# Raw weight tiles fetched by transfers that GpSimd issues instead of SP

## The chip, the cores and the metric

The kernel runs on one core of a Trainium2 chip. The metric is the device time of one execution in microseconds (us). The core has TensorE (PE in the profile; PEld is its weight load), VectorE (DVE), ScalarE (ACT), GpSimd (POOL) and SyncE (SP). Each of them takes its own instructions strictly in order and waits on semaphores for the others. A transfer between HBM and SBUF is an instruction in the queue of the engine that issues it; the data is then moved by 16 DMA engines that all queues share.

## The reference

A small encoder trunk of two layers is run on two requests, of 1024 and 512 tokens, with one set of weights, all in float32.

```
def attn_retention_layer(x, g, w_in, qk_gain, ret_decay, w_out):
    z = rmsnorm(x, g) @ w_in
    qa, ka, va, ga, qb, kb, vb, gb = jnp.split(z, cuts, axis=-1)
    ...
    oa = dense_gqa(qa, ka, va)                         # mixer A, after norm and rotary
    ob = rmsnorm(fwd + bwd, None)                      # mixer B, retention in both directions
    mixed = jnp.concatenate([jax.nn.silu(ga) * oa, jax.nn.silu(gb) * ob], axis=-1)
    return x + mixed @ w_out
def windowed_layer(x, g, w_in, sink, rel_bias, w_out):
    z = rmsnorm(x, g) @ w_in
    q, k, v, gate = jnp.split(z, [...], axis=-1)
    o = banded_sink_gqa(q, k, v, sink, rel_bias)       # mixer C, +-128 tokens
    return x + (jax.nn.silu(gate) * o) @ w_out
```

The trunk applies the first layer, then the second, then a last RMS norm.

## The kernel before, in words

The 1536 tokens are 12 blocks of 128, in three groups t of four blocks (512 tokens). Activations stay in SBUF with the model dimension on the partitions, as a high part and a low part (tiles `xh` and `xl`, 8 of each per group, float32r). The weights are split the same way, and a product is three matmuls: high times high, high times low, low times high.

A weight matrix comes from HBM in chunks of 256 output columns. `load_w` (line 130) fetches one chunk in four pieces. For each piece it takes a raw tile `wraw` of 128 x 512 float32 (256 KB, 2 buffers in all), starts a transfer into it (line 134), makes the high part on GpSimd (line 136) and the low part (line 137) into a tile `w` or `wg`. The low part is made on GpSimd, except where the caller passes `lo=nc.vector`: then on VectorE. Once line 137 has read the raw tile, its buffer is free for the next transfer but one. There are 44 chunks, so 176 raw tiles.

Transfers of nearly everything else go through SP too: loads of activations, of residuals and of parked results (`mo`, `y`, `yn`, `xr`), and stores of gates, branch outputs and results. Twelve transfers, the keys and values of the attention, are issued by GpSimd already (lines 760 and 416).

In order of time (of the profiled execution):
- 0 to 116 us: the input is loaded and scaled (GpSimd scales groups t = 1 and 2 into `xh`, line 107), then the key, value and query projections of mixer A, with rotary steps on GpSimd (lines 103 and 394).
- 116 to 310: mixer B.
- 310 to 810: attention of mixer A; the scores of later blocks run beside the products of earlier ones, and between them fill matmuls of the gate projections (`psg`), from about 617 us on of the output projection of groups 2 and 0 (`pso`, function `out_proj_fm`). There GpSimd also multiplies branch output by gate (`mo`, line 259), sums squares (`acc`, line 282), and from about 740 us scales group 2 (`yn`, line 805).
- 810 to 887: the output projection of group 1 (`out_proj`, low parts on VectorE) and the key and value projection of mixer C.
- 887 to 1310: attention of mixer C with its query and gate projections as fill.
- 1310 to 1542: output projection of layer 1 (low parts on VectorE throughout), first beside the last attention units, from about 1430 us alone, and the final norm.

What stands in which order on each engine is decided when the program is built: a scheduler places every instruction by its own estimate of durations and by priorities, and it gives each tile a buffer. So one edit shifts rows all over the program. Between engines only semaphores decide.

Of the kernel before, what the change touches and what calls it, by code (L numbers as in the profile page):

```python
# [36 lines left out]
def trunk_kernel(ctx, tc, x, xT, wab, woab, wc, woc, gT, qkg, ret, sink, relb, fng,  # L37
                 ropeA, ropeB, dist, kdist, qdist, onehot, wmask, out_p0, out_p1, out_s):
    nc = tc.nc
    dma = nc.sync.dma_start  # L40
# [12 lines left out]
    def buf(tag, name, n=None, dt=F32):  # L53
        t = wk.tile([P, SIZE[tag]], dt, tag=tag, name=name, bufs=BUFS[tag])
        return t if n is None else t[:, :n]
# [74 lines left out]
    def load_w(arr, c, tag, lo=None, hook=None, ks=range(KT)):  # L130
        ts = {}
        for i in (k // 2 for k in ks[::2]):
            raw = wp.tile([P, 2 * CW], F32, tag="wraw", name="wraw", bufs=2)
            dma(out=raw, in_=arr[c, :, 2 * i:2 * i + 2, :].rearrange("p k n -> p (k n)"))
            w = wp.tile([P, 2, 2 * CW], F32R, tag=tag, name=tag, bufs=4)
            nc.gpsimd.tensor_scalar(w[:, 0, :], raw, 1.0, 1.0, ALU.mult, ALU.mult)  # L136
            (lo or nc.gpsimd).tensor_tensor(w[:, 1, :], raw, w[:, 0, :].bitcast(F32), ALU.subtract)  # L137
            ts[i] = w
            if hook is not None:
                hook(i)  # L140

        def get(s, k, a=0, n=CW):
            o = (k % 2) * CW + a
            return ts[k // 2][:, s, o:o + n]
        return get
# [76 lines left out]
    def gate_stream(warr, c0, gd, scale=None):  # L222
        for c in range(4):
            w = load_w(warr, c0 + c, "wg")
            for t in ORDER:
                for j in range(2):
                    yield from gate_pieces(w, j, 2 * c + j, t, gd, scale)
# [35 lines left out]
    def out_proj_fm(t, warr, ks, res, dst, finish, prev, lo):  # L263
        acc = buf("T", "acc")
        for c in range(4):
            w = load_w(warr, c, "w", lo, None, ks)
            for a in range(2):
                k = 2 * c + a
                y, sq = stage("y")
                dma(out=y, in_=res(k))  # L270
                ps = ps_p("pso")
                for kk in ks:
                    proj_fm_k(ps, w, a * P, t, kk, ks)
                    if kk != ks[-1]:
                        yield
                for side in ahead[:1] + (prev or []):
                    next(side, None)
                nc.vector.tensor_tensor(y, ps, y, ALU.add)
                dma(out=dst[k][t], in_=y)
                nc.scalar.activation(sq if k else acc, y, AF.Square)  # L280
                if k:
                    nc.gpsimd.tensor_tensor(acc, acc, sq, ALU.add)
                yield
# [32 lines left out]
    def out_proj(t, warr, ks, res, finish):  # L316
        x1 = [load_block(res(t * GB + j), "xr") for j in range(GB)]
        for c in range(4):
            with tc.high_priority():
                w = load_w(warr, c, "wg" if c % 2 else "w", nc.vector, None, ks)  # L320
            for j in range(GB):
                ps = ps_any("pso")[:, :CW]
                proj_tm(ps, w, t * GB + j, ks)
                sl = x1[j][c // 2][:, (c % 2) * CW:(c % 2 + 1) * CW]
                with tc.high_priority():
                    nc.vector.tensor_tensor(sl, ps, sl, ALU.add)
        finish(t, x1)
# [10 lines left out]
    sp_d = {(n, g, i): dr.tile([P, 1024 if i == 0 else 512], F32, name=f"sp{n}{g}{i}")[:]  # L338
            for n in ("ak", "av", "ch", "cl", "cv") for g in range(2) for i in range(2)}

# [1 line left out]
    ident = const.tile([P, P], F32, name="ident")  # L342
    make_identity(nc, ident)
    nhalf = const.tile([P, 8], F32, name="nhalf")
# [16 lines left out]
        for b in range(t * GB, t * GB + GB):  # L361
            block_rstd(load_block(x[b], "xb", "H"), rs[:, b:b + 1])

# [1 line left out]
    dma(out=g_sb, in_=gT)  # L365
    nc.scalar.activation(rs, rs, AF.Tanh)
    wkv = load_w(wab, 4, "w", None, lambda i: [load_xt(0, k) for k in ((0, 1), (2, 3, 4, 5), (6, 7), ())[i]])
# [127 lines left out]
        if p % 2:  # L495
            kv_group(p // 2)

# [1 line left out]
    ropeb = buf("S4", "ropeb").rearrange("p (f b d) -> p f b d", f=2, b=8)  # L499
    dma(out=ropeb, in_=ropeB)  # L500
    qdec = buf("S4", "qdec").rearrange("p (h a i) -> p h a i", h=4, a=2)
# [116 lines left out]
            tail, last = retention(h, w, b0, b1), tail  # L618
            last()

# [1 line left out]
    class Back:  # L622
        def __init__(self, eget, n, vget, od, k0, t, j, gd):
            self.n, self.eget, self.vget, self.od, self.k0, self.t, self.j = n, eget, vget, od, k0, t, j
# [46 lines left out]
                split(X["h", k, self.t][:, sl], X["l", k, self.t][:, sl], oT[:, a, :], 0.5)  # L671

    def pipeline(units, prep, front, cap, frees, rate, fill, hook, before=None):
        """Software pipeline: the scores of later units run beside the products of this one, as far as
        the buffers of the exponentials (cap of them) reach."""
        n = len(units)
        st_ = dict(u=0, gen=None, live=0)
        ctxs, backs, pend = {0: prep(units[0])}, {}, []

        def advance():  # L680
            u = st_["u"]
            if u >= n:
                return False
            if st_["gen"] is None:
                st_["gen"] = front(units[u], ctxs.pop(u))
                if u + 1 < n:
                    ctxs[u + 1] = prep(units[u + 1])
                st_["need"] = next(st_["gen"])
            if st_["live"] + st_["need"] > cap:
                return False  # L690
            st_["live"] += st_["need"]
            try:
                st_["need"] = next(st_["gen"])
            except StopIteration as e:
                backs[u] = e.value
                st_["u"], st_["gen"] = u + 1, None
            return True

        credit = 0.0
        for u in range(n):  # L700
            while u not in backs:
                advance()
                if before is not None and backs:
                    before()
                    before = None
            back = backs.pop(u)
            for kb in range(back.n):
                back.T(kb)
                st_["live"] -= frees(kb, back.n)
                credit = min(credit + rate(back.n), 4.0)  # L710
                while credit >= 1.0 and advance():
                    credit -= 1.0
                fill.step()
                for f in pend:
                    f()
                pend = [lambda bk=back, kb=kb: bk.PV(kb)]
                if kb == 0:
                    hook(units[u])
        for f in pend:
            f()  # L720
# [79 lines left out]
                    lambda kb: load_a("av", g, b)[:, kb * P:(kb + 1) * P], o_ab, 2 * g, t, j,  # L800
                    g_ab if g == 1 and t < 2 else None)

# [1 line left out]
    def fin_fm(t, k, y, rb):  # L804
        nc.gpsimd.tensor_tensor(y, y, rb, ALU.mult)
        split_x(y, k, t, g_sb[:, KT + k:KT + k + 1])
# [43 lines left out]

    out_proj(1, woab, KS_A, lambda b: x[b], fin_ab)

# [1 line left out]
    wkv = load_w(wc, 0, "w")  # L854
    kd_raw = {}
    for p in PAIRS:
# [34 lines left out]
            split(q[r0:r0 + 64], q[r1:r1 + 64], ps[r0:r0 + 64], 0.125)  # L891
        yield

# [1 line left out]
    k_c, v_c = {0: (KH, KL)}, {0: (V,)}  # L895
    qs = {}
    bias_c = {}
# [104 lines left out]
        return Back(lambda h, kb: es[h][:, kb * P:(kb + 1) * P], k1 - k0, lambda kb: vget_c(c, k0 + kb), o_c, 2 * c, t, j,  # L1002
                    g_c if (c, t) == (3, 1) else None)

# [1 line left out]
    def fin_out(t, k, y, rb):  # L1006
        nc.vector.scalar_tensor_tensor(y, y, g_sb[:, 2 * KT + k:2 * KT + k + 1], rb, ALU.mult, ALU.mult)
        dma(out=(out_p0, None, out_s)[t][k], in_=y)
# [126 lines left out]
```

## Time and profile before

| | |
|---|---|
| median of three runs | 1546.78 us (1539.06, 1546.78, 1547.49) |
| span of the profiled execution, first to last instruction | 1541.9 us (its whole time is not listed apart from the three runs) |
| busy PE / PEld | 1467.9 us (95%) / 1277.2 us (83%) |
| busy DVE / ACT / POOL | 1061.1 (69%) / 714.0 (46%) / 804.7 us (52%) |
| transfers | 179.54 MB, mean 116 GB/s |
| raw weight tiles | 176 transfers of 256 KB, all issued by SP, 3.2 to 3.6 us from issue to landing |
| granted TensorE clock, mean | 0.985 |

Busy shares are means over stages with different limits. DMA-issuing instructions are not counted as busy time, those on GpSimd neither, although one of them holds the engine for as long as it lasts.

### The profile page before, as it was taken

To read this page: it belongs to the slowest core of one execution; us is meant where nothing else is said; L and a number is where in the kernel's file an instruction comes from. 1 tells how busy PE (TensorE), PEld (TensorE's weight loads), DVE (VectorE), ACT (ScalarE), POOL (GpSimd) and SP (SyncE) were. 2 spreads that over 40 slices of the span, in tenths; PEclk is the share of its full clock that TensorE was granted. 3 is DMA by queue.
4 is the path that set the end of the run, shared out by engine and by line. 5 is a ranking of instruction groups with operands and counts; after the bars stand their busy time and mean duration, and the time that the engine had idled before them with its cause. 6 is when DMAs were issued, how large, how long until landed. Compare 5 with 4: busy or idle time off the path is not lost.

```text
span 1541.9 us, 26034 instructions
## 1 busy us (share of the span) xinstructions
PE 1467.9 (95%) x8746; PEld 1277.2 (83%) x8746; DVE 1061.1 (69%) x2488; ACT 714.0 (46%) x1768; POOL 804.7 (52%) x1040
## 2 busy tenths in 40 slices
PE   7989999989999999999998999999999999988897
PEld 7988999987888888778777998888888888766677
DVE  6596455578667667877888327677777767898554
ACT  3632222245455555655653235556556556555102
POOL 7783334257456374887896414442522432567433
PEclk9998999999999999999999999999999999999999
DMA  9441011224421132654563422112213211567773
GB/s 334 155 154 52 19 45 49 64 85 140 138 73 59 48 110 73 217 166 130 153 218 115 124 78 78 52 57 56 80 49 93 61 53 52 169 211 235 242 247 123
DMA packets 112662, 179.54 MB, mean 116 GB/s; under 512 B 12880, under 2 KB 34000, under 8 KB 112528
## 3 DMA queue, kind: packets, MB, share of 16 engines
q1 hardware_dynamic: 110512, 172.37, 35.6%
q0 software_dynamic: 2016, 5.51, 1.2%
q8 instruction: 69, 1.13, 0.3%
q14 instruction: 65, 0.53, 0.1%
HBM read 125.63 MB, written 56.39 MB: 118 GB/s over the span
## 4 chain that ended last, share of the span: by engine, by line
PE 65%; DVE 12%; DMA 8%; POOL 5%; issue 4%; ACT 2%; SPq 1%; POOLq 0%; DVEq 0%; ACTq 0%
PE psg L89 16%; PE psq L89 10%; PE psb L89 8%; PE po L89 8%; PE pte L170 6%; PE pso L89 4%; PE sc L89 3%; PE s L89 3%; PE pskv L89 2%; DMA wraw<-in_woc 2%; DVE xl L118 1%; DVE w L137 1%; DVE nm L782 1%; DMA wraw<-in_woab 1%; DVE el L112 1%
## 5 line engine op out<-in xcount | busy, mean ns | idle before, releaser
L89 PE MATMUL psg<-xh,wg 128*128 128x512 f32 x768 | 261.6, 399 | 1.4 <-POOL wg L137 1.2
L112 DVE TENSOR_TENSOR el<-pte,eh 128x512 fp32r<-128x512 f32 x288 | 196.6, 684 | 56.7 <-ACT eh L111 29.6
L107 POOL TENSOR_SCALAR ec<-ec,rl 128x384 f32<-128x384 f32 (+1 forms) x192 | 109.0, 582 | 233.0 <-DVE rl L997 77.1
L111 ACT ACTIVATE eh<-pte 128x512 fp32r<-128x512 f32 x288 | 169.4, 596 | 119.6 <-PE po L89 66.4
L89 PE MATMUL pso<-xh,w 128*128 128x512 f32 x512 | 179.8, 409 | 9.8 <-DVE w L137 4.3
L89 PEld LDWEIGHTS psg<-xh,wg 128*128 128x128 f32 x768 | 143.7, 188 | 29.7 <-POOL wg L137 1.6
L107 POOL TENSOR_SCALAR e<-e,rl 128x512 f32<-128x512 f32 x160 | 114.6, 728 | 81.7 <-DVE rl L793 23.8
L89 PE MATMUL psg<-xl,wg 128*128 128x512 f32 x384 | 151.1, 393 | 0.0
L992 ACT ACTIVATE ec<-ec,nm 128x384 f32<-128x384 f32 (+1 forms) x192 | 109.6, 572 | 85.6 <-DVE nm L990 80.8
L790 ACT ACTIVATE e<-s,nm 128x512 f32<-128x512 f32 x160 | 108.9, 687 | 75.3 <-DVE nm L787 56.1
L136 POOL TENSOR_SCALAR w<-wraw 128x512 fp32r<-128x512 f32 x116 | 78.7, 680 | 117.7 <-DMA wraw<-in_woc 35.2
L782 DVE TENSOR_REDUCE nm<-s 128x1 f32<-128x512 f32 x160 | 107.5, 682 | 34.3 <-PE s L89 34.0
L89 PE MATMUL psq<-xh,w 128*128 128x512 f32 x384 | 130.1, 397 | 0.6 <-DVE oT L655 0.6
L89 PEld LDWEIGHTS pso<-xh,w 128*128 128x128 f32 x512 | 96.1, 191 | 34.7 <-DVE w L137 7.8
L986 DVE CUSTOM_DVE_ANT_0 ec<-sc,bias,sink_s 128x384 f32<-128x384 f32 (+1 forms) x192 | 105.2, 568 | 20.3 <-PE sc L89 17.4
L89 PE MATMUL pso<-xl,w 128*128 128x512 f32 x256 | 102.0, 399 | 3.3 <-DVE xl L118 3.3
L170 PEld LDWEIGHTS pte<-ident,e 128*128 128x128 f32 x640 | 78.4, 142 | 20.5 <-ACT e L790 1.7
L170 PE MATMUL pte<-ident,e 128*128 128x128 f32 x640 | 94.6, 275 | 0.8 <-ACT e L790 0.6
L137 POOL TENSOR_TENSOR w<-wraw,w 128x512 fp32r<-128x512 f32 x68 | 90.5, 1335 | 1.8
L89 PEld LDWEIGHTS psq<-xh,w 128*128 128x128 f32 x384 | 71.8, 188 | 14.4 <-PE po L89 0.9
L89 PEld LDWEIGHTS psg<-xl,wg 128*128 128x128 f32 x384 | 72.3, 188 | 13.2
L89 PE MATMUL pskv<-w,xh 128*128 128x256 f32 x384 | 73.3, 293 | 9.0 <-ACT xh L117 6.7
(225 smaller groups left out, 3981.8 us busy)
## 6 DMA issues: line engine op xcount, KB each, us to landing
wraw<-in_woab SPq DMA_DIRECT2D x48, 256.0 KB, 3.3
wraw<-in_woc SPq DMA_DIRECT2D x48, 256.0 KB, 3.6
wraw<-in_wab SPq DMA_DIRECT2D x44, 256.0 KB, 3.3
wraw<-in_wc SPq DMA_DIRECT2D x36, 256.0 KB, 3.2
xt<-in_xT SPq DMA_DIRECT2D x24, 256.0 KB, 5.3
xb<-in_x SPq DMA_DIRECT2D x24, 256.0 KB, 4.9
qd<-qdw SPq DMA_DIRECT2D x24, 256.0 KB, 2.0
qd<-qd SPq DMA_DIRECT2D x24, 256.0 KB, 3.1
```

The source lines that it names most:

```text
L89: i = nc.tensor.matmul(ps, lhsT=lhsT, rhs=rhs, start=start, stop=stop)
L107: nc.gpsimd.tensor_scalar(o, i, s, 1.0, ALU.mult, ALU.mult)
L111: nc.scalar.activation(hi, src, AF.Copy)
L112: nc.vector.tensor_tensor(lo, src, hi.bitcast(F32), ALU.subtract)
L118: nc.vector.scalar_tensor_tensor(lo, src, scale, hi.bitcast(F32), ALU.mult, ALU.subtract)
L136: nc.gpsimd.tensor_scalar(w[:, 0, :], raw, 1.0, 1.0, ALU.mult, ALU.mult)
L137: (lo or nc.gpsimd).tensor_tensor(w[:, 1, :], raw, w[:, 0, :].bitcast(F32), ALU.subtract)
L170: return nc.tensor.transpose(o, i, ident)
L782: nc.vector.tensor_reduce(nm2[:, c:c + 1] if nh == 2 else nm[:, h:h + 1], s, AX.X, ALU.max, negate=True)
L790: nc.scalar.activation(eh[c], ss[c], AF.Exp, bias=nm[:, h:h + 1], accum_out=l[:, h, c:c + 1])
L986: nc.vector.tensor_tensor_reduce(es[h][:, :nk], s, bias[h][:, bo:bo + nk], 1.0, sink_s[:, 4 * c + h:4 * c + h + 1], ALU.add, ALU.max, mx[: ...
L992: nc.scalar.activation(es[a][:, :nk], es[a][:, :nk], AF.Exp, bias=nm[:, a:a + 1], accum_out=l[:, a:a + 1])
```

## The change

In `load_w` the transfer into the raw tile is issued by GpSimd (`nc.gpsimd.dma_start`) and no longer by SP (`dma` is `nc.sync.dma_start`). Size, source, buffers and all arithmetic stay. Some comment lines and a docstring go as well.

```
@@ -131,7 +131,7 @@
         ts = {}
         for i in (k // 2 for k in ks[::2]):
             raw = wp.tile([P, 2 * CW], F32, tag="wraw", name="wraw", bufs=2)
-            dma(out=raw, in_=arr[c, :, 2 * i:2 * i + 2, :].rearrange("p k n -> p (k n)"))
+            nc.gpsimd.dma_start(out=raw, in_=arr[c, :, 2 * i:2 * i + 2, :].rearrange("p k n -> p (k n)"))
             w = wp.tile([P, 2, 2 * CW], F32R, tag=tag, name=tag, bufs=4)
             nc.gpsimd.tensor_scalar(w[:, 0, :], raw, 1.0, 1.0, ALU.mult, ALU.mult)
             (lo or nc.gpsimd).tensor_tensor(w[:, 1, :], raw, w[:, 0, :].bitcast(F32), ALU.subtract)
```

The scheduler draws the whole program anew. SP has 176 rows fewer, GpSimd 176 more.

First place: GpSimd in the output projection of layer 0, group 0 (about 770 us). `e` are exponentials of the attention, which TensorE waits for; `w_9522` and `w_9527` are two pieces of one chunk, `wraw_9530` and `wraw_9535` the raw tiles of the next two. GpSimd before:

```order
L136 TENSOR_SCALAR w_9522<-wraw_9520 128x512 [waits DMAHW0_49,PE_49]
L107 TENSOR_SCALAR e_9150<-e_9150,rl_9048 128x512 [waits DVE_49,Activation_49]
L107 TENSOR_SCALAR e_9151<-e_9151,rl_9048 128x512 [waits Activation_49]
L137 TENSOR_TENSOR w_9522<-wraw_9520,w_9522 128x512 [waits Pool_49]
L259 TENSOR_TENSOR mo_9501<-mo_9501 128x512 [waits DMAHW4_49,DMAHW3_49]
L666 TENSOR_TENSOR oT_9185<-oT_9185,gq_9188 128x256 [waits DVE_49]
L136 TENSOR_SCALAR w_9527<-wraw_9525 128x512 [waits DMAHW2_49,PE_49]
L805 TENSOR_TENSOR yn_9509<-yn_9509,rb_8925 128x512 [waits DMAHW5_49,DVE_49]
L282 TENSOR_TENSOR acc_8927<-acc_8927,y_9251 128x512 [waits Activation_49]
L136 TENSOR_SCALAR w_9532<-wraw_9530 128x512 [waits DMAHW7_49,PE_49]
```

GpSimd in the changed kernel:

```order
L137 TENSOR_TENSOR w_9522<-wraw_9520,w_9522 128x512 [waits Pool_49]
L259 TENSOR_TENSOR mo_9501<-mo_9501 128x512 [waits DMAHW7_49,DMAHW6_49,DVE_49]
L805 TENSOR_TENSOR yn_9509<-yn_9509,rb_8925 128x512 [waits DMAHW0_49,DVE_49]
L137 TENSOR_TENSOR w_9527<-wraw_9525,w_9527 128x512 [waits Pool_49]
L134 DMA wraw_9530<-in_woab 128x512 [waits Pool_49]
L107 TENSOR_SCALAR e_9296<-e_9296,rl_9048 128x512 [waits DVE_49,PE_49,Activation_49]
L107 TENSOR_SCALAR e_9297<-e_9297,rl_9048 128x512 [waits PE_49,Activation_49]
L107 TENSOR_SCALAR e_9314<-e_9314,rl_9048 128x512 [waits DVE_49,PE_49,Activation_49]
L107 TENSOR_SCALAR e_9315<-e_9315,rl_9048 128x512 [waits PE_49,Activation_49]
L282 TENSOR_TENSOR acc_8927<-acc_8927,y_9381 128x512 [waits Activation_49]
L134 DMA wraw_9535<-in_woab 128x512 [waits Pool_49]
L259 TENSOR_TENSOR mo_9648<-mo_9648 128x512 [waits DMAHW7_49,DMAHW6_49,DVE_49]
```

The transfers now stand in GpSimd's own row, between the multiplications, ahead of the exponentials' scaling; where before one stood on SP, GpSimd went on at once.

Second place: GpSimd in the last output projection (about 1505 to 1520 us), where VectorE makes the low parts. The names are pieces of the last two chunks. GpSimd before:

```order
L136 TENSOR_SCALAR w_17868<-wraw_17866 128x512 [waits DMAHW5_49]
L136 TENSOR_SCALAR w_17873<-wraw_17871 128x512 [waits DMAHW3_49]
L1036 TENSOR_TENSOR xr0_17602<-xr0_17602,fn_17600 128x512 [waits Activation_49]
L136 TENSOR_SCALAR w_17878<-wraw_17876 128x512 [waits DMAHW7_49,PE_49]
L136 TENSOR_SCALAR w_17883<-wraw_17881 128x512 [waits DMAHW0_49,PE_49,Pool_49]
L136 TENSOR_SCALAR wg_17992<-wraw_17990 128x512 [waits DMAHW1_49,PE_49,Pool_49]
```

GpSimd in the changed kernel:

```order
L134 DMA wraw_17871<-in_woc 128x512 [waits DVE_49]
L134 DMA wraw_17876<-in_woc 128x512 [waits DVE_49]
L136 TENSOR_SCALAR w_17873<-wraw_17871 128x512 [waits DMASW7_49,PE_49]
L136 TENSOR_SCALAR w_17878<-wraw_17876 128x512 [waits DMASW0_49,PE_49]
L134 DMA wraw_17881<-in_woc 128x512 [waits DVE_49]
L1036 TENSOR_TENSOR xr0_17602<-xr0_17602,fn_17600 128x512 [waits Activation_49]
L134 DMA wraw_17990<-in_woc 128x512 [waits DVE_49]
L136 TENSOR_SCALAR w_17883<-wraw_17881 128x512 [waits DMASW1_49,PE_49]
```

Each transfer now waits on GpSimd for VectorE to free the raw tile, and the next splitting step stands behind it.

## Rows read from the trace of the kernel before

**Rows 1.** The page: busy time, share of the span, instructions of each engine.
```profile
PE 1467.9 (95%) x8746; PEld 1277.2 (83%) x8746; DVE 1061.1 (69%) x2488; ACT 714.0 (46%) x1768; POOL 804.7 (52%) x1040
```

**Rows 2.** Stretches: length, then busy us of PE, PEld, DVE, ACT, POOL, clock, DMA.
```profile
0.00:38.50 38.50, 28.20 (x198) 27.32 (x199) 24.04 (x32) 15.08 (x31) 30.32 (x40) 0.96 0.95 335
38.50:115.60 77.10, 72.32 (x587) 71.08 (x587) 58.17 (x146) 37.57 (x113) 59.94 (x72) 0.98 0.48 155
115.60:616.80 501.20, 488.32 (x3150) 435.75 (x3150) 321.04 (x701) 210.53 (x467) 241.59 (x352) 0.98 0.24 73
616.80:809.50 192.70, 184.82 (x928) 147.32 (x927) 158.17 (x291) 111.39 (x252) 160.93 (x167) 0.99 0.57 177
809.50:886.60 77.10, 68.52 (x517) 64.88 (x517) 43.93 (x75) 23.06 (x55) 44.86 (x50) 0.98 0.40 119
886.60:1310.60 424.00, 423.08 (x2285) 363.12 (x2284) 291.24 (x917) 236.37 (x656) 148.89 (x228) 1.00 0.22 65
1310.60:1426.30 115.70, 104.39 (x497) 82.39 (x496) 101.62 (x230) 62.34 (x156) 74.85 (x83) 0.99 0.64 205
1426.30:1541.90 115.60, 98.26 (x596) 85.34 (x595) 62.92 (x101) 17.71 (x43) 43.27 (x52) 0.95 0.64 204
```

**Rows 3.** Raw-tile transfers by stretch (0:115.6, 616.8:809.5, 809.5:886.6, 1310.6:1426.3, 1426.3:1541.9): median us to landing.
```profile
wraw<-in_wab SPq DMA_DIRECT2D x18, 256.0 KB, 4.0
...
wraw<-in_woab SPq DMA_DIRECT2D x27, 256.0 KB, 3.8
...
wraw<-in_woab SPq DMA_DIRECT2D x15, 256.0 KB, 3.3
wraw<-in_wc SPq DMA_DIRECT2D x6, 256.0 KB, 3.3
...
wraw<-in_woc SPq DMA_DIRECT2D x18, 256.0 KB, 3.6
...
wraw<-in_woc SPq DMA_DIRECT2D x28, 256.0 KB, 3.9
```

**Rows 4.** Tiles ak and wraw: issuing instructions, duration ns min/median/max.
```profile
L760 POOL DMA_DIRECT2D ak<-spak x4: 540/628/771, 281.7 to 548.5; - x4
...
L134 SPq DMA_DIRECT2D wraw<-in_woc x48: 327/333/422, 1236.6 to 1517.4; - x48
```

**Rows 5.** Chain of waits, about 784 to 802 us: start, us, what.
```profile
789.83 1.20 POOL oT L666
791.03 1.50 POOL e L107 x2
...
796.23 2.54 POOL w L137 x2
...
800.45 1.26 POOL acc L282
```

**Rows 6.** Transfers issued in 281:283, then in 381:392.
```profile
ak<-spak POOLq DMA_DIRECT2D x1, 256.0 KB, 3.2
...
btabd<-browd SPq DMA_DIRECT2D x1, 4096.0 KB, 18.0
...
gab<-gz SPq DMA_DIRECT2D x1, 256.0 KB, 15.7
av<-spav POOLq DMA_DIRECT2D x1, 256.0 KB, 9.1
```

**Rows 7.** Issue times: SP in 370:410, GpSimd in 372:402 (start, us).
```profile
381.42 0.64 SPq L610 DMA_DIRECT2D btabd<-browd  x1
...
385.32 0.50 SPq L219 DMA_DIRECT2D gab<-gz  x1
...
390.85 0.61 POOL L760 DMA_DIRECT2D av<-spav  x1 [7.70 <-PE po L89]
```

**Rows 8.** Waits of SP's queue: us in total, times, longest.
```profile
SPq L134 <- POOL w L137: 151.4, 51, 22.6
...
SPq L134 <- POOL wg L137: 91.7, 39, 22.3
...
SPq L134 <- DVE w L137: 43.4, 33, 3.7
```

**Rows 9.** Waits of PEld: us in total, times, longest.
```profile
PEld pso L89 <- POOL w L136: 12.0, 11, 2.5
PEld pso L89 <- DVE w L137: 9.1, 13, 3.1
PEld pskv L89 <- POOL w L136: 7.9, 2, 6.7
```

More of the change, by code (lines that the diff above doesn't have):

```diff
@@ L133, in load_w @@
             raw = wp.tile([P, 2 * CW], F32, tag="wraw", name="wraw", bufs=2)
-            dma(out=raw, in_=arr[c, :, 2 * i:2 * i + 2, :].rearrange("p k n -> p (k n)"))
+            nc.gpsimd.dma_start(out=raw, in_=arr[c, :, 2 * i:2 * i + 2, :].rearrange("p k n -> p (k n)"))
             w = wp.tile([P, 2, 2 * CW], F32R, tag=tag, name=tag, bufs=4)
```

## The prediction

> **What bounds the kernel now.** I read four views in this order. First the busy table of the page: TensorE works 1467.9 of 1541.9 us, GpSimd 804.7 [rows 1]. So at most 74 us stand open on TensorE in all, and GpSimd as a mean has room. Second the stretches, since the mean hides the stages [rows 2]. Between 887 and 1310 us TensorE misses one microsecond in 424, and GpSimd is busy 149: nothing done to GpSimd there, within reason, can move the end. From 116 to 617 us GpSimd is busy 242 of 501. What is to be seen is where GpSimd is *not* free: 30.3 of 38.5 us at the start, 59.9 of 77.1 in the projections of mixer A, 160.9 of 192.7 (84%) beside the output projection of layer 0. From 1311 to 1426 VectorE is the full one (101.6 of 115.7), and after 1426 no engine but TensorE is near its limit. Third the chain of waits: at 790 us it runs on GpSimd, through `oT`, `e`, `w`, `acc` [rows 5] (the group shows four pieces; from 786 to 802 it does not leave GpSimd). There GpSimd sets the end. Fourth the waits on weights: TensorE's weight load stood 12.0 + 9.1 + 7.9 = 29.0 us for split weight tiles, of which one wait of 6.7 is the start of the program [rows 9]. So 22 us is the most that a better supply of weights could give back.
>
> **The change, part by part.**
>
> *Removed from SP:* 176 issues of 0.33 us [rows 4], and the waits in front of them: 151.4 + 91.7 + 43.4 = 286.5 us in which SP stood for a raw buffer while other transfers were queued behind [rows 8]. Those transfers are loads of `mo`, `y`, `yn` and `xr` and stores of gates and results. That sounds large, but SP has its own time, and what was queued behind is ordered by the same scheduler to be early. The gain shows only where TensorE waited for something that SP brought late; the 22 us above are an upper bound for weights, and I find nothing of that size for the other loads.
>
> *Added to GpSimd:* 176 issues. The four issues of `ak` took 540 to 771 ns, median 628 [rows 4]; I take 0.63 us. In total 176 x 0.63 = 111 us, which brings GpSimd to 916 of 1542 us, 59%. By stage, with the counts of [rows 3] and the busy times of [rows 2]:
> - 0 to 115.6 us: 18 x 0.63 = 11.3 us. Busy goes from 90.3 to 101.6 of 115.6.
> - 616.8 to 809.5: 27 x 0.63 = 17.0. Busy goes from 160.9 to 177.9 of 192.7, 92%.
> - 809.5 to 886.6: 21 x 0.63 = 13.2, from 44.9 to 58.1 of 77.1.
> - 1310.6 to 1426.3: 18 x 0.63 = 11.3, from 74.9 to 86.2 of 115.7.
> - 1426.3 to the end: 28 x 0.63 = 17.6, from 43.3 to 60.9 of 115.6.
> - the other 64: 40 us, in stretches where GpSimd has over 250 us free each. Nothing.
>
> *A wait that moves:* where VectorE makes the low part, the issue waits for VectorE on GpSimd's queue. SP stood 43.4 us in 33 such waits [rows 8], 1.3 us each; behind the waiting issue now stand the scaling of exponentials, the product `mo`, and the next splitting step, for which TensorE waits. Between 1311 and 1426 that is 18 x 1.3 = 23 us, and GpSimd's 86.2 become 109.6 of 115.7 in the worst case; in the best the scheduler has placed the issues where VectorE is done already (it puts other steps between), and nothing is added.
>
> *Landing:* SP's raw tiles landed 3.3 to 4.0 us after issue by stage medians [rows 3]. A transfer of the same size issued by GpSimd in a quiet moment landed after 3.2 us [rows 6]. So no loss and no gain in flight. A queue of its own could let a raw tile pass a backlog on SP's. At 381.42 us SP started a 4 MB copy that landed 18.0 us later, at 399.4. The 256 KB store `gab` that SP issued at 385.32 landed at 401.0, and `av`, of the same size, that GpSimd issued at 390.85, at 400.0 [rows 6, 7]. Issued 5.5 us later, it overtook by one microsecond: both waited for the big copy. So I allow the separate queue no more than about 1 us for a tile, and only where the DMA engines are full.
>
> The Trainium skill says the same from the other side: "DMA: Bandwidth & Descriptors", section "Issuing engines are not separate DMA queues", has transfers of all issuers run on the same 16 engines, so that several issuers save only the issue time. By that rule the change frees 0.33 us of SP for each 0.63 us of GpSimd that it takes. The trace agrees by the 9.1 us that `av` took beside SP's copy [rows 6].
>
> *What reaches the end.* In the stretches above I take a share of the added time by how near GpSimd is to its limit.
> - Start and projections: between 0 and 11.3. Input scaling and rotary steps run on GpSimd at 78%, but TensorE has work of its own beside them. I take 3.
> - 617 to 809: between 0 and 17.0. Four raw tiles are issued in the stretch 784 to 802 where the chain is on GpSimd, 2.5 us straight on the path; before it, GpSimd has 31.8 us free in 192.7, which the 17.0 halve, so some of the backlog is carried to the end. I take 5.
> - 809 to 887: the supply of weights is in step with landing, split and release. Between 0 and 13.2; the issues fall mostly where GpSimd waits for a raw tile anyway. I take 2.
> - 1311 to 1426: between 0 and 11.3 + 23 = 34. VectorE stays the bound. I take 2.
> - 1426 to the end: GpSimd waits there more than it works. 28 tiles, of which SP held some behind loads that waited; between a gain of 13, a half of the 12.0 + 9.1 us of rows 9 and 2 more for overtaking, and a loss of 17.6. I take a gain of 2.
>
> Sum: 3 + 5 + 2 + 2 - 2 = +10 us, 1541.9 to about 1552 in the span. The median run lies 1546.8 - 1541.9 = 4.9 above the profiled span, so the forecast in the metric is 1552 + 5 = 1557 us, 0.66% more.
>
> **The rivals.**
>
> *A, the forecast:* GpSimd's issue time reaches the end in the three stages where GpSimd is over 75% busy. Its own range is +2 to +22, 1549 to 1569.
>
> *B, hidden anyway:* the scheduler knows of the issues and sets them into gaps. For it speaks that GpSimd has 737 us free as a whole and that TensorE waits little on it outside the chain at 790 us. Against it that in 617 to 809 only 31.8 us are free, in pieces. It gives 0 +- 6: 1547.
>
> *C, SP is unblocked and weights come sooner:* of the 22 us of TensorE's waits for weights [rows 9], a half goes, and of the loads behind SP's 286.5 us of standing some come earlier. For it: in the last 116 us TensorE is open for 17 us and the chain there passes through landings of raw tiles. Against it: the raw buffer is free only when GpSimd or VectorE has split the tile, and that is not changed. It gives -12: 1535.
>
> *D, GpSimd becomes the bound:* in 617 to 809 its queue fills, since each issue also stands in front of the exponentials' scaling (first place of the order rows), and from 1311 on the issues stand for VectorE. From the point at which GpSimd's free time in a stage is under the added time plus its unavoidable waits (half of the 31.8 in 617 to 809, as a guess), each further issue is on the path. Price: 17.0 there, 11.3 at the start, and a third of 34 late, 11: +40, 1587.
>
> The Trainium skill has a rule that would make D worse: "SBUF — State Buffer", section "SBUF: two separate sides", says that a transfer issued by GpSimd has its descriptors written by GpSimd's cores, which VectorE locks out during some of its operations. The rows that bear on it are the four issues of `ak`, the longest 0.77 us [rows 4], with VectorE 64% busy in their stretch [rows 2]. So far they don't show such a stall.
>
> That the change doesn't do what it says I leave out: 176 rows do move.
>
> **How the numbers follow.** Chances: A 0.42, B 0.25, C 0.22, D 0.11. About 0.5% (7.7 us) is what a measurement of this kernel can tell from no change. Slower by more: D, and a little under two thirds of A (its middle is 10, its lower part is under 7.7), 0.11 + 0.26, with 0.03 of B, 0.40. Faster: most of C with a little of B, 0.22. Within: the rest, 0.38. The likeliest case is A, so 1557. For the range I go down into C, to 1534, and up into D, to 1582, which leaves out about 0.1 on either side. Signs are mixed, so A's own range, 1549 to 1569, stands beside it.
>
> **What would show it.** Issues of raw tiles on GpSimd of 0.5 to 0.8 us, 176 of them: then the price is right; a median over 1 us would put D in front. In the stretch of the output projection of layer 0, GpSimd at over 90% and the stretch some 5 us longer, with TensorE waiting for exponentials or `mo`: A. The same length with GpSimd fuller: B. In the last 116 us TensorE's waits on weights well under the 12 us of before and landings under 3.5 us: C. The attention of mixer C (424 us) must stay as it is; if it moves by more than 3 us, the new order of rows, and not the issuer, is at work, and all the sums above are beside the point. The prediction is wrong if the time falls by over 8 us, or if the loss lies in the stages where GpSimd is free.

## The result and the profile after

The changed kernel takes 1593.7 us (median of 4 runs, 1586.9 to 1595.6) where the kernel before took 1545.1 beside it. The ratio is 1.0318, with a 95% interval of 1.0287 to 1.0349: 3.2% slower. The forecast was 1557 us, its range 1534 to 1582. The profiled run took 1586.9 us, its span is 1585.1, 43.2 more than before. All of the parts below are made against that span.

The busy line of the page after, which answers to [rows 1]:

```profile
PE 1481.5 (93%) x8746; PEld 1289.0 (81%) x8746; DVE 1082.4 (68%) x2488; ACT 710.9 (45%) x1768; POOL 893.2 (56%) x1216
```

GpSimd has the 176 issues more, and is still open for 692 us. Other than was said of the page of before, this row counts issues on GpSimd as busy time: 1216 less 1040 is 176, and the 1040 of before have 14 issues among them (not twelve). TensorE does the same 8746 matmuls and is busy 13.6 us longer; the other 29.6 us it stands. VectorE, which does the same 2488 instructions, is busy 21.3 us longer.

The stretches of [rows 2], the first two as one, cut after at the places where TensorE has done the same number of matmuls (length, then busy us of PE, PEld, DVE, ACT, POOL, then clock, DMA share, GB/s):

```profile
0.00:122.00 122.00, 104.27 (x783) 101.13 (x784) 88.78 (x169) 49.93 (x135) 97.63 (x124) 0.99 0.56 194
122.00:624.50 502.50, 488.32 (x3151) 435.85 (x3150) 325.52 (x711) 212.13 (x478) 258.10 (x388) 0.98 0.24 75
624.50:821.80 197.30, 182.75 (x928) 145.16 (x927) 168.84 (x297) 113.07 (x259) 170.22 (x189) 1.00 0.54 171
821.80:910.50 88.70, 74.81 (x519) 70.77 (x518) 40.78 (x64) 16.29 (x40) 60.41 (x77) 0.88 0.34 104
910.50:1339.00 428.50, 425.12 (x2285) 363.94 (x2284) 296.87 (x920) 239.60 (x661) 167.01 (x263) 1.00 0.21 64
1339.00:1456.10 117.10, 105.17 (x497) 84.27 (x496) 103.29 (x236) 63.25 (x159) 82.03 (x99) 0.96 0.60 201
1456.10:1585.10 129.00, 101.02 (x596) 87.83 (x595) 58.29 (x95) 16.62 (x40) 57.83 (x80) 0.91 0.57 184
```

Less the lengths of [rows 2], the seven stretches are longer by 6.4, 1.3, 4.6, 11.6, 4.5, 1.4 and 13.4 us. The loss lies at the start and around the output projections of both layers, and 25 of the 43 us lie in two stretches, 809.5 to 886.6 and 1426.3 to the end. The matmuls don't come in the same order in both kernels, so a place moves by some us when it is told by one tile: near 809.5 us of before, the attention's `po` is 5.3 us late, and the feature-major output projection, whose last matmul ends at 813.2, is 20.1 late. (In a feature-major projection, `out_proj_fm`, the result has the model dimension on the partitions; in a token-major one, `out_proj`, the tokens.)

In the stretch 624.5 to 821.8 TensorE stands 14.6 us (7.9 before). None of its waits listed there ends on GpSimd; the two longest groups end on VectorE:

```profile
PE pte L170 <- DVE el L112: 3.1, 3, 2.2
PE s L89 <- DVE el L112: 2.2, 2, 2.0
```

VectorE is busy 10.7 us longer there. Its 29 `nm` of 128 x 1 (line 787) take 728 ns in the mean where they took 473. The shortest take 0.14; those over 0.5 us end, nearly all, within 0.03 us of the end of a GpSimd instruction with two inputs (more in the last section).

*The issue itself.* The rows of the tile `wraw` after (duration in ns, minimum, median, maximum), which answer to [rows 4], with the landing in us:

```profile
L134 POOL DMA_DIRECT2D wraw<-in_woab x48: 536/584/622, 572.6 to 886.6; - x48
...
DMA to landing us min/median/max: 3.2/3.6/6.9
```

The price was read rightly: 0.58 us against 0.63 taken, and no issue of any group is over 0.743. The same landing row of before reads 2.9/3.3/6.5, so a tile is some 0.3 us longer under way. The Trainium skill, "DMA: Bandwidth & Descriptors", "Issuing engine by pattern", gives plain loads to SyncE and calls its path generally the faster one. The two medians agree in direction.

*When the issue comes.* In before, two low parts that GpSimd makes in layer 0 (start, us, what):

```profile
783.02 1.60 POOL L137 TENSOR_TENSOR w<-wraw,w 128x512 fp32r<-128x512 f32 x1
...
788.59 1.29 POOL L137 TENSOR_TENSOR w<-wraw,w 128x512 fp32r<-128x512 f32 x1
```

and SP's issues at that place:

```profile
784.65 0.33 SPq L134 DMA_DIRECT2D wraw<-in_woab  x1
789.91 0.33 SPq L134 DMA_DIRECT2D wraw<-in_woab  x1
```

The low part ends at 784.62 and 789.88; SP, which has been standing for it, sends the next tile 0.03 us later. The same place after, on GpSimd:

```profile
798.04 1.72 POOL L137 TENSOR_TENSOR w<-wraw,w 128x512 fp32r<-128x512 f32 x1
799.74 1.79 POOL L107 TENSOR_SCALAR e<-e,rl 128x512 f32<-128x512 f32 x2
801.50 1.42 POOL L137 TENSOR_TENSOR w<-wraw,w 128x512 fp32r<-128x512 f32 x1
802.88 1.34 POOL L259 TENSOR_TENSOR mo<-mo 128x512 f32<-128x512 f32 x1
804.18 1.29 POOL L805 TENSOR_TENSOR yn<-yn,rb 128x512 f32<-128x512 f32 x1
805.41 0.58 POOL L134 DMA_DIRECT2D wraw<-in_woab  x1
```

The first buffer is free at 799.76, the issue starts at 805.41: 5.6 us late, behind `e`, `w`, `mo` and `yn`. No view of waits shows this, since GpSimd never stands. Taken for all tiles (start of an issue less the end of the low part of the tile two before it, as there are two buffers), the median delay is 0.03 us before and 1.10 after; in layer 0's feature-major groups it is 2.0 and 2.3.

*What follows from late tiles.* GpSimd at the end of layer 0's feature-major work, before:

```profile
824.64 0.63 POOL L136 TENSOR_SCALAR wg<-wraw 128x512 fp32r<-128x512 f32 x1 [2.36 <-issue]
826.46 0.62 POOL L136 TENSOR_SCALAR wg<-wraw 128x512 fp32r<-128x512 f32 x1 [1.19 <-DVE xr L326]
830.70 0.63 POOL L136 TENSOR_SCALAR wg<-wraw 128x512 fp32r<-128x512 f32 x1 [2.59 <-PE R L89]
831.33 11.46 POOL L805 TENSOR_TENSOR yn<-yn,rb 128x512 f32<-128x512 f32 x7
```

and after:

```profile
844.36 0.61 POOL L136 TENSOR_SCALAR wg<-wraw 128x512 fp32r<-128x512 f32 x1
846.33 1.15 POOL L134 DMA_DIRECT2D wraw<-in_woab  x2 [1.37 <-DVE w L137]
848.43 12.19 POOL L805 TENSOR_TENSOR yn<-yn,rb 128x512 f32<-128x512 f32 x8 [0.95 <-ACT rb L295]
860.60 2.06 POOL L136 TENSOR_SCALAR wg<-wraw 128x512 fp32r<-128x512 f32 x2
```

with TensorE's row behind it:

```profile
861.70 1.01 PE L89 MATMUL pso<-wg,xh 128*128 128x256 f32 x3 [7.16 <-POOL wg L136]
```

Both kernels have a block of `yn` products here. Before, a whole chunk's four tiles were split ahead of it (the first at 821.66), and TensorE had work beside most of it. After, one tile of that chunk is split; the next two are issued at 846.3, and their split stands behind 12.2 us of `yn`. TensorE stands 7.16 us for it. Its clock follows, by the windows around:

```profile
840.00:850.00 10.00, 10.00 (x63) 10.00 (x63) 4.26 (x10) 0.84 (x2) 5.24 (x8) 0.68 0.35 104
860.00:870.00 10.00, 7.75 (x46) 7.46 (x47) 5.85 (x7) 0.72 (x1) 5.58 (x9) 0.66 0.19 52
```

The granted clock of 0.68 and 0.66 means the lower of the two levels (1.2 GHz) for a good part of each window, the first after TensorE had stood twice for over 1 us between 835 and 838.3, the second after the 7.16. In the stretch 821.8 to 910.5 TensorE stands 13.9 us (8.6 before), so 5.3 of the 11.6 us are standing. The other 6.3 are longer busy time for as many matmuls, at a granted clock of 0.88 in the mean where it was 0.98.

*The last stretch.* TensorE's weight load, 1457 to the end, against 8.4 and 3.4 us for the first and last of these rows in before's stretch:

```profile
PEld pso L89 <- POOL w L136: 14.6, 11, 3.2
PEld pso L89 <- DVE wg L137: 3.2, 1, 3.2
PEld pso L89 <- DVE w L137: 2.8, 6, 1.0
```

For the last 16 raw tiles the time from one free buffer to the next (delay, issue, landing, split) is 5.9 us in the mean before and 6.5 after; the 0.6 more are the delay of the issue (0.06 and 0.66). With two buffers that makes a tile every 2.9 and every 3.2 us, and so they come: 2.88 and 3.19 us apart. These 16 tiles alone lose about 5 us.

### The profile page after: what moved, and what is told of

Read it like the earlier page. It is cut to its first block, busy times and chain, and to the rows that moved or that the text cites. A ratio compares the mean times of both kernels' runs of the same rounds, so it can differ in the third digit from the quotient of the medians.

```text
span 1585.1 us, 25975 instructions
## 1 busy us (share of the span) xinstructions
PE 1481.5 (93%) x8746; PEld 1289.0 (81%) x8746; DVE 1082.4 (68%) x2488; ACT 710.9 (45%) x1768; POOL 893.2 (56%) x1216
## 4 chain that ended last, share of the span: by engine, by line
PE 64%; DVE 15%; DMA 10%; issue 5%; POOL 3%; ACT 2%; SPq 0%; POOLq 0%; DVEq 0%; ACTq 0%
PE psg L89 15%; PE psq L89 8%; PE pso L89 8%; PE po L89 8%; PE psb L89 7%; PE pte L170 6%; PE sc L89 3%; PE s L89 3%; DVE xl L118 2%; PE pskv L89 2%; DVE nm L782 2%; DVE el L112 2%; DMA xt<-in_xT 1%; DMA wraw<-in_woab 1%; DVE qdw L400 1%
## 5 line engine op out<-in xcount | busy, mean ns | idle before, releaser
L89 PE MATMUL pso<-xh,w 128*128 128x512 f32 x512 | 179.3, 411 | 13.6 <-POOL w L136 11.8
L89 PEld LDWEIGHTS pso<-xh,w 128*128 128x128 f32 x512 | 96.6, 193 | 39.3 <-POOL w L136 15.3
L89 PE MATMUL pskv<-w,xh 128*128 128x256 f32 x384 | 76.6, 301 | 9.3 <-POOL w L136 7.7
```

The costliest lines, as they stand in the source:

```text
L89: i = nc.tensor.matmul(ps, lhsT=lhsT, rhs=rhs, start=start, stop=stop)
```

## The experiments

The theories: **L** (late), a raw tile leaves late because its issue has a place in GpSimd's queue; **T** (time), the 0.59 us of each issue on an engine that is full; **F**, freeing SP or a new order of rows does harm; **I**, transfers that GpSimd issues are slower themselves or held up. In the edits below, long arguments are cut to `...`. All ratios are to the kernel before on the same chip.

To read a run by stage, the table below gives how far TensorE is behind the profile of before, in us, when it has done the same matmuls: the eighth part of `pskv` (23.6 us before), all of `psb` (288.3), seven eighths of `s` (730.9), all of `pskv` (916.0), all of `sc` (1400.7) and all of `pso` (1532.7). Each is the end of that matmul in one timeline less its end in before's. For one profile each, and with another order of rows in each kernel, differences of 2 or 3 us say little.

```
                                       23.6   288.3   730.9   916.0  1400.7  1532.7
changed kernel                         +5.4    +7.1    +6.1   +23.8   +24.8   +40.1
e1  ScalarE issues                     -1.6    -0.4    -1.2    +0.2    +0.8    +0.3
e2  SP issues, GpSimd clears 512       +3.6    +0.2    +3.2   +14.1   +22.9   +27.8
e10 SP issues, GpSimd clears 1         +0.5    -4.2    +0.2    +7.6   +10.8   +14.9
e3  changed, 5 raw buffers in one part +5.3    +6.8    +5.4   +12.8   +17.3   +32.9
e9  changed, issue at high priority    +3.8    +4.9    +3.1   +17.3   +19.9   +37.1
e5  GpSimd: first 8 tiles              +3.8    -2.1    -0.8    -0.2    -0.9    -4.1
e6  GpSimd: feature-major 64           +2.3    +1.9    +1.2   +18.5   +12.8   +27.0
e7  GpSimd: token-major 32             +2.5    +2.3    +2.2    -2.2    -3.9    +0.2
e8  GpSimd: the other 72               -0.1    -2.3    +1.5    +1.0    +3.6    +4.5
e11 GpSimd: both projections 96        +1.5    +0.7    +0.9   +23.7   +18.6   +37.3
e14 less e13: third raw buffer         +7.8    +6.0   +10.4   +19.7   +20.0   +21.0
e16 less e15: low parts on VectorE     +3.7    +1.9    +3.9    +7.5   +15.2   +31.0
```

**e1, another issuer.**

```diff
-            nc.gpsimd.dma_start(out=raw, in_=arr[c, ...])
+            nc.scalar.dma_start(out=raw, in_=arr[c, ...])
```

> The 176 raw tiles are issued by ScalarE in place of GpSimd. Theory L (late): the loss of 48.6 us is that a raw tile's issue stands in the in-order queue of an engine that computes, behind its work and behind its waits, so that it leaves later than SP would send it; ScalarE computes too (45% busy), so a good part of the loss stays: 1565 to 1590. Theory T (time): it is the 0.59 us of GpSimd for each issue, in stages where GpSimd is nearly full; ScalarE has the room, so most of it goes: 1545 to 1555. Theory F (freeing SP harms or the order of rows does): as after, 1585 to 1600.

1547.2 us, ratio 1.0028 (1.0010 to 1.0047). ScalarE's issue takes what SP's takes:

```profile
L134 ACTq DMA_DIRECT2D wraw<-in_woab x48: 334/334/365, 560.0 to 862.5; - x48
```

T's range holds (1545 to 1555), L's and F's do not. Freeing SP does no harm: with SP freed of the same 176 issues next to nothing is lost. A new order of rows need not cost anything either, though this order is not that of the changed kernel. L as I put it here is out too: a computing engine's queue alone does not make the issue late. On ScalarE the median delay behind a free buffer is 0.03 us, as on SP. The loss belongs to GpSimd, the engine that also makes the splits that free the buffer.

**e2 and e10, GpSimd's place with and without time.** SP issues as before; GpSimd clears the buffer first, in e2 all of it, in e10 one column.

```diff
+            nc.gpsimd.memset(raw, 0.0)            # e2;  e10: raw[:, 0:1]
             dma(out=raw, in_=arr[c, ...])
```

> As before, SP issues; but GpSimd first clears each raw buffer (128x512), so the tile needs a place in GpSimd's queue and some of its time ahead of SP's issue, without a DMA issued by GpSimd. Theories L and T both say that the loss comes back: 1580 to 1610 (T: in proportion to the time of a clear, L: whatever it takes). Theory I (issuer): GpSimd's transfers themselves are slower in flight or held up; then it is 1545 to 1560.

> As the run with the cleared buffers (SP issues), but GpSimd clears one column of a raw buffer in place of 512: the place in its queue stays, nearly all of the 0.53 us go. There the loss was 27 to 29 us. Theory L: it stays over 15 us, 1560 to 1575. Theory T: it falls to a fifth, 1545 to 1551.

The clears (ns), first of e2, then of e10:

```profile
L134 POOL MEMSET wraw<- x176: 515/526/542, 0.9 to 1546.4; 128x512 f32 x176
```

```profile
L134 POOL MEMSET wraw<- x176: 88/98/124, 0.9 to 1533.5; 128x1 f32 x176
```

e2: 1571.2 us, 1.0181 (1.0152 to 1.0210), 29 us. e10: 1556.7, 1.0087 (1.0063 to 1.0111), 14 us. No transfer of these tiles is issued by GpSimd, and over half of the loss is there, so I alone cannot be it. What is missing to the 49 us can still be I's. The 27 to 29 us of e2 were below what L and T expected (1580 to 1610). e10 falls between the two expectations: with a fifth of the time, half of the loss stays. Place and time both count, each for about 14 us of e2's. In e10 the issue comes as late as in the changed kernel (median 1.17 us behind a free buffer, 2.2 and 2.7 in layer 0's feature-major groups, against 1.10, 2.0 and 2.3), and that costs 14 us, not 49. So by these runs a late issue by itself is the smaller part of the loss.

**e3 and e4, five raw buffers in the token-major projections.**

```diff
-            raw = wp.tile([P, 2 * CW], F32, tag="wraw", name="wraw", bufs=2)
+            raw = buf("S2", "wraw") if more and i % 2 else wp.tile([P, 2 * CW], F32, tag="wraw", name="wraw", bufs=2)
```

> The changed kernel, with five raw buffers in place of two in the token-major output projections only (every second raw tile in a buffer of the tag S2, which is idle there). What the two stages lost against before is about 8 and 4 us. Theory L: with five buffers the issue no longer waits for VectorE's split, tiles are fetched ahead, and that comes back: 1580 to 1586. Theory T: GpSimd's time is the same, nothing comes back: 1590 to 1597.

> The kernel before, with the same five raw buffers in the token-major output projections: the control. Theory L: TensorE waits little for raw tiles there with SP as issuer, so 1540 to 1547. Theory T: 1545, no change.

e3: 1580.3 us, 1.0255 (1.0204 to 1.0306). That is 13 us less than the changed kernel, 10 by the two ratios; their intervals overlap a little, since one of e3's four runs took 1593.0. e4: 1543.0, 1.0004 (0.9985 to 1.0023), no change. Both are in L's ranges. The table says where: 10 us are regained between 731 and 916. TensorE's longest wait in the stretch 830 to 916 of the changed kernel:

```profile
PE pso L89 <- POOL wg L136: 9.5, 2, 7.2
```

and all of its waits in 826 to 909 of e3:

```profile
PE pso L89 <- DVE xr L326: 2.1, 1, 2.1
PE po L89 <- DVE el L112: 1.5, 1, 1.5
PE pso L89 <- POOL w L136: 0.6, 1, 0.6
PE pso L89 <- DVE w L137: 0.5, 1, 0.5
```

In layer 1 nothing more comes back; nearly all that e3 loses there it loses ahead of the token-major part.

**e5 to e8, one part of the loads each,** and **e11, two of them.** `load_w` takes the issuer as an argument, and only the calls named pass GpSimd's:

```diff
-            dma(out=raw, in_=arr[c, ...])
+            dq(out=raw, in_=arr[c, ...])          # dq=nc.gpsimd.dma_start in the calls named
```

> GpSimd issues only the 8 raw tiles of the first two loads (keys and values, first queries of mixer A); SP the other 168. The changed kernel is 5 to 7 us behind at 30 us and stays so. If the parts add up, this one costs 5 to 7: 1547 to 1550.

> GpSimd issues only the raw tiles of the feature-major output projections (64 tiles: groups 2 and 0 of both layers). By the points where the changed kernel falls behind, about 13 us in layer 0 and 9 in layer 1: 1560 to 1566. Theory T has it all here, since GpSimd is at 84 to 92% only beside these projections in layer 0: up to 1575. If nothing comes, the loss needs the tiles of other loads: 1545.

> GpSimd issues only the raw tiles of the token-major output projections (32 tiles). Theory L: the supply of raw tiles by two buffers gets slower than TensorE's use of them, 10 to 14 us: 1552 to 1556. Theory T: GpSimd has time there (58 of 77 us at most), 0 to 4: 1542 to 1546.

> GpSimd issues only the raw tiles that neither the first two loads nor the output projections use (72: retention, later queries, gates, mixer C). The changed kernel loses nothing visible between 116 and 700 us, 1 to 4 between 890 and 1330: 1542 to 1547. Over 1552 would say that the order of rows elsewhere costs.

> GpSimd issues the raw tiles of both kinds of output projection (96), SP the other 80. Alone the feature-major ones cost 25 us and the token-major ones 1. If they add: 1568 to 1574. Theory L has them work together: without split tiles in hand from the group before, a token-major projection feels each late tile, 5 and 7 us more (the places where the changed kernel falls behind the one with the feature-major tiles alone): 1578 to 1588.

e5: 1540.9, 0.9969 (0.9956 to 0.9982). e6: 1569.7, 1.0149 (1.0110 to 1.0188). e7: 1545.8, 1.0008 (0.9994 to 1.0022). e8: 1551.3, 1.0043 (1.0023 to 1.0062). The ranges of e5 (1547 to 1550) and e8 (1542 to 1547) were missed, and e6 came above the first of its ranges, under T's 1575. e11: 1587.9, 1.0296 (1.0272 to 1.0320).

The feature-major groups carry the loss, -4, +25, +1 and +6 us. But the parts add up to 28, not to 49, and e11 shows where the rest is: the token-major tiles cost 1 us alone and some 20 more where the feature-major ones are late too. L's number for e11 (1578 to 1588) holds, the added one (1568 to 1574) does not. For e7 T's number held and L's did not. In layer 0 the reading is that a token-major projection starts with split tiles in hand, and only without them feels each late tile: e7 loses nothing there (+2.2 at 731, -2.2 at 916), while e11 is 5.2 us behind e6 at 916. In layer 1 it does not hold: e7 is level at the end only because it is 3.9 us ahead at 1400.7, and loses 4.1 from there, with its token-major tiles alone. e5 is 3.8 us behind at 24 us and ahead at 288, so the changed kernel's 6 to 7 us there are not the first eight tiles alone; what they are was not tried.

**e9, the issue at high priority.**

```diff
+            with tc.high_priority():
-            nc.gpsimd.dma_start(out=raw, in_=arr[c, ...])
+                nc.gpsimd.dma_start(out=raw, in_=arr[c, ...])
```

> The changed kernel, with the issue of a raw tile at high priority: the scheduler puts it on GpSimd as soon as the buffer is free, ahead of other work, at the same 0.59 us. In the changed kernel it stood 2.1 and 2.7 us after its buffer was free in the two feature-major groups of layer 0, where SP took 0.4 and 0.6. Theory L, the place: the delay falls under 1.2 us and most of the loss behind 735 us comes back, 1550 to 1570. Theory T, the time: the 0.59 us stay on GpSimd, 1585 to 1600. If the delay stays, it is the work before the issue that frees the buffer, and the run tells nothing on the time.

1593.1 us, 1.0325 (1.0287 to 1.0362). The median delay stayed, 1.09 us, and 1.9 and 2.2 in layer 0's feature-major groups, so as said beforehand it tells nothing on the time. The order of GpSimd's rows did change, but the place of the issue is not to be had by a priority here.

**e13 and e14, a third raw buffer everywhere,** paid for with one of the twelve `E` buffers.

```diff
-    BUFS = dict(E=12, S4=3, ...
+    BUFS = dict(E=11, S4=3, ...
-            raw = wp.tile([P, 2 * CW], F32, tag="wraw", name="wraw", bufs=2)
+            raw = wp.tile([P, 2 * CW], F32, tag="wraw", name="wraw", bufs=3)
```

> The kernel before, with a third raw buffer everywhere, paid for with one of the twelve buffers of the tag E. The control for the next one: 1540 to 1560, whatever the theory (the missing buffer of E may cost something in the attention).

> The changed kernel with the same third raw buffer. Theory L: a tile that is asked for 2 to 3 us late is asked for a tile earlier, so most of the loss goes: 5 to 20 us over the control. Theory T: GpSimd's 0.59 us for each issue are still there, 40 to 50 us over the control.

e13: 1605.5 us, 1.0374 (1.0336 to 1.0412); e14: 1627.8, 1.0515 (1.0473 to 1.0557), 22 us over its control, just above L's 5 to 20 and far from T's 40 to 50. The control missed its range: the smaller `E` costs 60 us. But that lies in mixer C's attention (1.8 us behind at 916, 78 at 1400.7), so the other stages can still be compared. Between 1400.7 and 1532.7 the change costs 1 us with three buffers (20.0 to 21.0) where it cost 15 with two (24.8 to 40.1). TensorE's waits from 1425 to the end, the longest of the changed kernel:

```profile
PE pso L89 <- POOL w L136: 12.4, 10, 3.1
PE pso L89 <- DVE wg L137: 3.0, 1, 3.0
```

and with the third buffer, from 1470 to the end:

```profile
PE po L89 <- DVE el L112: 7.7, 2, 4.9
PE pso L89 <- DVE w L137: 5.6, 3, 2.3
PE pso L89 <- DVE xr L326: 1.8, 1, 1.8
```

The first kind of wait, on the high part that comes when the tile lands, is gone. So in the last stretch the loss is that the loop of two buffers got longer. Whether by the delay, by the time of the issue or by the order of rows this run can't tell, since a third buffer covers each of them; e10, with the delay and hardly any time, loses 4.1 us there and e2 4.9, the changed kernel 15.3. In layer 0 the third buffer helps less: 731 to 916 still costs 9.3 us, of 17.7.

**e15 and e16, other work taken off GpSimd in layer 0:** the low parts of the feature-major groups are made by VectorE.

```diff
-            fill.gens.append(out_proj_fm(t, woab, ..., None if t else late, None))
+            fill.gens.append(out_proj_fm(t, woab, ..., None if t else late, nc.vector))
```

> The kernel before, with the low parts of the weights of layer 0's feature-major groups made by VectorE (0.69 us) in place of GpSimd (1.29 us), 32 of them. The control for the next one: 1540 to 1555.

> The changed kernel with the same edit: between 560 and 830 us GpSimd has 41 us less to do, more than the 32 issues (19 us) put on it. If its being full there makes the loss of layer 0 (about 13 us up to the end of the feature-major groups), that part goes: 28 to 38 us over the control. If it is the place of the issue behind the split that frees the buffer, 43 to 52 over the control.

e15: 1557.3 us, 1.0068 (1.0047 to 1.0089); e16: 1593.4, 1.0297 (1.0262 to 1.0332), 36 us over its control. The control is 2 us over its range, since VectorE has 32 low parts more to make there: TensorE is 10.4 us behind at 731 and 17.5 at 916. Against it the change costs 3.6 us from 731 to 916, where it cost 17.7; from 1401 to 1533, where nothing was edited, 15.8, as before (15.3). So in layer 0 most of the loss goes when the splits leave GpSimd, as expected of a full engine. But three things change at once: GpSimd has 41 us less to do, the issue no longer stands behind the split that frees its buffer (its median delay falls to 1.05 and 0.30 us in the two groups), and 32 of GpSimd's instructions with two inputs, which can hold VectorE up (last section), are gone. And the control itself loses 7.1 us in that stretch, which may cover some. That it is time more than place is not shown: e10 loses 7.4 us there with a clear of 0.10 us, e2 10.9 with one of 0.53. As a way out it is none: e16 is no faster than the changed kernel.

**e12, a version that might beat both:** e5's issuer for the first eight tiles and e4's five buffers.

> A version that might beat both: GpSimd issues only the first 8 raw tiles (that alone was 0.3% faster), and the token-major output projections have five raw buffers (that alone changed nothing). If the 0.3% are of the start, they stay: 1538 to 1543. If they were the luck of one order of rows, 1543 to 1550.

1537.9 us, 0.9970 (0.9958 to 0.9982), at the lower edge of the first range: 0.3% faster than before, and by the two ratios 3.4% faster than the changed kernel. e5 alone gives the same 0.3%, so the buffers add nothing to it. Whether it is the issuer or the rows that it moves stays open: by the same matmuls (`psb`) e5 is 6.9 us behind at 109 us and 2.0 ahead at 142, when its eight issues (the last before 50 us) are long over.

## Why the prediction was wrong

*Right.* The bound and the direction; the price of an issue (0.58 us for 0.63); the landing (no loss worth a term); SP's relief gains nothing, as e1 shows, so C falls; mixer B and the attention of mixer A up to 617 us stay (+1.3 us in 501). One small step of the sum is off: the 4.9 us from span to metric hold some spread between runs, for in every listed run of the two kernels the time is 1.8 us over its span.

*The start, +3 forecast.* +6.4. The working's bounds held it (0 to 11.3).

*617 to 809, +5 forecast.* +4.6 at the same number of matmuls. That is near in number only. What is seen there is not a path through GpSimd, but TensorE waiting for VectorE; and the feature-major projection is 20.1 us late at its end, which comes due in the next stretch.

*809 to 887, +2 forecast.* +11.6, and here the step failed. The term leant on "the issues fall mostly where GpSimd waits for a raw tile anyway". Such a GpSimd is idle because it is one station of the loop issue, landing, split, release, with two buffers in it. An issue put into a loop lengthens it, however idle its engine; and the working counted only the issue's time (13.2 us at most), not the delay with which it comes. With five buffers 10 us between 731 and 916 come back (e3). The cover that hid the loss of layer 0 in e7, split tiles in hand, is by e11 what the late feature-major groups had used up, and TensorE's lower clock is 6.3 of the 11.6 us.

*1426 to the end, -2 forecast.* +13.4, the worst term, and the sign. "GpSimd waits there more than it works" was read as room; it is the same loop. GpSimd is busy 57.8 us of 129.0 there, its issues counted, and TensorE stands all the same. With a third buffer in the loop the change costs 1 us (e14).

*The attention of mixer C, nothing forecast.* +4.5 in 424 us: 2.5 of standing and 2.0 of longer busy time, nearly all of it before 1040 us (by the tiles of the table, from the end of `pskv` to that of `sc`, it is +1.0). That is over the 3 us that I had named as the sign of the new order of rows, so the order of rows is not excluded as a part of the loss.

*The rivals.* D's number, 1587, is nearest, and D had 0.11. That is luck: D put 17.0 us into 617 to 809, where 4.6 came, and 11 into 1311 to 1426, where 1.4 came, and nothing into the two stretches that lost most, in which GpSimd was busy 58% and 37% before. No rival had the longer loop as a cost. Of the signs that I named, the last one tells it: the loss lies in the stages where GpSimd is free. A's sign failed: 617 to 809 is 4.6 us longer, but at 86% of GpSimd and not over 90%.

*What stays open.* 6 us of the start; the 4.5 of mixer C; how time and place divide in layer 0; and how the last 20 us between e2 and the changed kernel divide between the issue's longer path, VectorE's 21 us and the order of rows, which differs in every kernel here. VectorE's extra time goes with issues on GpSimd and not with their place: it is busy 1082.4 us in the changed kernel and 1061.1 before, but 1054.3 in e2 and 1059.1 in e10.

## What to carry to other kernels

Before a transfer's issue is given to an engine, find who frees the buffer and what stands in the engine's queue between that and the issue: SP computes nothing, and the 287 us that it stood in [rows 8] were what made it prompt. Idle time of an engine inside a loop with few buffers is not room; count the loop (issue, landing, split, release, over the number of buffers) and compare it with what the consumer takes for one tile. Costs of parts that share a cover do not add, so try the parts together as well.

## What the runs showed of the hardware

An issue of 256 KB takes 0.33 us on SP and on ScalarE, and 0.58 on GpSimd; no issue on GpSimd was seen to be held up by VectorE (the longest of the 176 took 0.74 us). It is the other way round that time was lost. After, on VectorE, at the place where the last `oT` is split in two pieces:

```profile
820.07 3.36 DVE L118 SCALAR_TENSOR_TENSOR xl<-oT,xh 128x128 fp32r<-128x128 f32 x2
```

and on GpSimd:

```profile
820.13 0.58 POOL L134 DMA_DIRECT2D wraw<-in_woab  x1
820.74 1.30 POOL L137 TENSOR_TENSOR w<-wraw,w 128x512 fp32r<-128x512 f32 x1
821.98 1.29 POOL L805 TENSOR_TENSOR yn<-yn,rb 128x512 f32<-128x512 f32 x1
```

The second piece starts at 820.27, within the issue, and ends at 823.43, behind both of GpSimd's instructions with two inputs; all 24 pieces take 0.50 us in the mean before and 0.71 after. 37 of VectorE's instructions without a PSUM operand began during an issue that such an instruction followed at once, and together took 24 us more than the shortest of their form; 66 that began during an issue with idle time behind it took 1 us more. The Trainium skill, "SBUF — State Buffer", "SBUF: two separate sides", has VectorE and GpSimd share a pair of ports, which VectorE wants for an instruction with two inputs in SBUF, among others; whoever starts first keeps it for its whole instruction. The rows agree that VectorE's piece waited for whole instructions with two inputs. They don't agree on who goes first: by the recorded starts the piece was 0.47 us ahead of GpSimd's first, and ended behind its second. For the issue itself they show no hold.
